# A decoder block in fp32: the MLP's normalized activations at 64 and at 0 modulo 128 bytes

## The chip, the core and the metric

One core of a Trainium2 chip runs the whole kernel. The metric is the device time of one execution in microseconds (us). TensorE (PE in the rows; its weight loads are listed apart as PEld) multiplies, VectorE (DVE) and ScalarE (ACT) do the elementwise work, GpSimd (POOL) helps, and SyncE (SP) issues the transfers.

## What is computed

A decoder block on 256 tokens of width 1024. Cut to the part at hand:

```python
h  = h + rmsnorm(m @ w_out, norm_mix_post)      # after two gated token mixers
u2 = rmsnorm(h, norm_mlp_pre)
a  = square(relu(u2 @ w_up))                    # w_up is 1024 x 4096
h  = h + rmsnorm(a @ w_down, norm_mlp_post)     # w_down is 4096 x 1024
```

## The kernel before, in words

Every fp32 matrix is split into a high and a low part (`..h`, `..l`) of the type fp32r, and each product is made of three matmuls: high by high, high by low and low by high (`mm3`, L223 to L229; `mm3_wide`, L231 to L240, does the same for a row that is 1024 wide). A matmul holds one operand, 128 columns of it, in the array: the stationary operand, which a weight load (LDWEIGHTS) of its own brings in. It then streams the other one, the moving operand, past it. Each matmul here has its weight load; the load for the next matmul runs while the present one streams.

Weights arrive by DMA (`.._r`), ScalarE makes the high part of a block (L89) and VectorE the low part (L93). The queues' orders are written out by hand.

The MLP works on eight chunks `j` of 512 hidden features. For chunks 1 to 7, `up_half` multiplies the weights `up{j}_h/l`, which are stationary, by the activations `u2h/u2l`, which are moving and 256 wide (all tokens): 2 halves x 2 feature tiles x 8 blocks of the contraction x 3 matmuls = 96 matmuls a chunk. The results are squared and split into `ah/al`, with which the down projection (`d_ps`) goes on: there `ah/al` are stationary and the weights `dn` move, 512 wide; the last step of each token tile in the chunks 0 to 5 has four matmuls that are only 256 wide (`mm3_narrow_end`, L250). Chunk 0 (`up_tokens`) is done the other way round: `u2h/u2l` stationary, the weights moving, 512 wide, 48 matmuls.

SBUF is allotted by pools, one tile after another. In the compiled program the address of a tile, in bytes within each partition, is fixed. Modulo 128 these are:

- all split weights (`up`, `dn`, `o`, `p`, `g`, ...): 96
- `uh/ul`, the first norm's activations, moving beside the weights of `q`, `k`, `p` and `g`: 32
- `u2h` and `u2l` (addresses 156,832 and 165,024): 32 and 32
- `ah/al`: 96, behind a tile `gap` of 64 bytes which holds nothing

`placed` makes a tile that is 128 elements too long and returns a view that begins `at` elements of 4 bytes behind its start; `uh/ul` come from it, `u2h/u2l` don't. Every step from one block of the contraction to the next, and every column slice that the matmuls take, is a multiple of 128 bytes, so that these residues hold for all operands of a tile.

Of the kernel before, what the change touches and what calls it, by code (L numbers as in the profile page):

```python
# [9 lines left out]
F32R = mybir.dt.float32r  # L10
# [6 lines left out]
P = 128  # L17
D = 1024
S = 256
NT = S // P  # L20
KD = D // P
# [12 lines left out]
def hybrid_block(ctx: ExitStack, tc: tile.TileContext, x, norm_mix_pre, w_in, b_gate, pool_w, pool_scale,  # L34
# [222 lines left out]
    def wide(blocks, k):  # L257
        b = blocks[k // 2]
        return b.hi[:, k % 2, :], b.lo[:, k % 2, :]
# [2 lines left out]
        b = blocks[k // 4]  # L262
        return b.hi[:, k % 4, c], b.lo[:, k % 4, c]

    def placed(pool, blocks, tag, name, at):


        t = pool.tile([P, blocks * S + 128], F32R, tag=tag, name=name)
        return t[:, at:at + blocks * S].rearrange("p (k s) -> p k s", k=blocks)

    def two(ps):
# [66 lines left out]

    v_sb = mixer.tile([P, NT, AW], F32, name="v_sb")
    u = tuple(placed(act, KD, f"uT_{i}", f"u{i}", 112) for i in "hl")  # L340
    rr = [const.tile([P, 1], F32, name=f"rr{t}") for t in range(NT)]

# [121 lines left out]
    stacked = mixer.tile([P, 2 * H * S + 32], F32R, tag="sg", name="stacked")  # L464
    k2, q2 = (stacked[:, a:a + H * S].rearrange("p (h s) -> p h s", h=H) for a in (0, H * S + 16))
    ql = [placed(mixer, 4, t, f"ql{i}", 112) for i, t in enumerate(("q_yh", "pt2"))]
    own = [slice(i * DH, (i + 1) * DH) for i in range(2)]

# [150 lines left out]
    def pool_project(g2):  # L619
        if not yp:  # L620
            yp.extend(placed(mixer, NG, t, t[2:], a) for t, a in (("q_yh", 32), ("k_yl", 48)))
        ps = bank(f"y_ps{g2}")
        for j in range(2):
            g = 2 * g2 + j
            mm3(ps[:, j * S:(j + 1) * S], (pws[0][:, g, :], pws[1][:, g, :]), (ys[0][:, g, :], ys[1][:, g, :]),
                True, True)
        for j in range(2):
            g = 2 * g2 + j
            v, sc = ps[:, j * S:(j + 1) * S], others[P_SCALE + g]
            nc.scalar.activation(yp[0][:, g, :], v, AF.Copy, scale=sc)  # L630
            nc.vector.scalar_tensor_tensor(yp[1][:, g, :], v, sc, yp[0][:, g, :].bitcast(F32),
                                           op0=ALU.mult, op1=ALU.subtract)
# [79 lines left out]
    for c in range(2):  # L712
        for f2 in range(2):
            f = 4 * c + 2 * f2
# [17 lines left out]
    mix.close()  # L732
    work = ctx.enter_context(tc.tile_pool(name="work", bufs=2))
    h_sb = work.tile([P, NT, D], F32, name="h_sb", bufs=1)
    u2 = tuple(work.tile([P, KD, S], F32R, name=f"u2{i}", bufs=1) for i in "hl")

    work.tile([P, 16], F32, name="gap", bufs=1)

# [52 lines left out]
    def squared_relu(ps, name):  # L791
        r = work.tile([P, 512], F32, tag="relu", name="relu" + name)
        nc.scalar.activation(r, ps, AF.Relu)  # L793
        a = work.tile([P, 512], F32, tag="a", name="a" + name)
        nc.vector.tensor_tensor(a, ps, r, ALU.mult)  # L795
        return a
# [48 lines left out]
    at = squared_relu(p0, "0_0")  # L845
# [5 lines left out]
    at = squared_relu(p1, "0_1")  # L851
# [78 lines left out]
    for n, c in halves():  # L930
        for k in range(4):
            h, l = wide(bd[-1], k)
# [31 lines left out]
```

## Time and profile before

| what | value |
|---|---|
| three runs, median (lowest to highest) | 340.08 us (339.73 to 341.2) |
| the profiled execution, its own time | 340.61 us |
| its span, from the first to the last instruction | 338.8 us |
| mean granted TensorE clock, share of full speed | 0.994 |
| TensorE busy / weight loads busy | 98% / 90% of the span |
| VectorE / ScalarE / GpSimd busy | 65% / 54% / 23% |

The profile describes one execution. The ends of matmuls are modelled and neighbours overlap, so the pace of TensorE is read from the distance between two starts, and not from the busy time of an instruction.

### The profile page before, as it was taken

How to read it: one execution, taken by the hardware profiler on the slowest of the kernel's cores; microseconds unless marked ns; L12 is line 12 of the kernel's file. 1: busy time of each engine (PE TensorE's matmuls, PEld its weight loads, DVE VectorE, ACT ScalarE, POOL GpSimd, SP SyncE). 2: the span in 40 equal slices, each digit the busy share in tenths (PEclk: the TensorE clock that was granted, in tenths of full speed). 3: DMA queues.
4: the chain of work that ended last, by engine and by line, in shares of the span. 5: the costliest groups of instructions: out<-in, count | busy, mean ns of one | idle time of the engine just before them, and what ended most of it. 6: DMA issues, size and time to landing. Idle time of an engine off the chain costs nothing.

```text
span 338.8 us, 5695 instructions
## 1 busy us (share of the span) xinstructions
PE 331.1 (98%) x2325; PEld 306.5 (90%) x2325; DVE 219.4 (65%) x288; ACT 182.3 (54%) x256; POOL 79.0 (23%) x68
## 2 busy tenths in 40 slices
PE   9999999999999999999999999999999999999992
PEld 7799999999999999888898998989989989899881
DVE  3799678996386799366686746637366374663535
ACT  3985677765746755076668526354264451544331
POOL 3699689145305000046700000000000000000000
PEclk9999999999999999999999999999999999999997
DMA  6996971654455946708355763917619267080003
GB/s 215 373 321 217 225 230 32 226 175 146 179 183 194 366 133 227 265 1 250 124 156 217 267 230 121 331 45 257 240 61 323 114 225 273 10 342 24 0 0 124
DMA packets 27362, 63.04 MB, mean 186 GB/s; under 512 B 1316, under 2 KB 2760, under 8 KB 27336
## 3 DMA queue, kind: packets, MB, share of 16 engines
q1 hardware_dynamic: 26760, 62.15, 53.4%
q0 software_dynamic: 576, 0.52, 1.2%
q8 instruction: 18, 0.29, 0.3%
q14 instruction: 8, 0.07, 0.1%
HBM read 61.10 MB, written 1.05 MB: 183 GB/s over the span
## 4 chain that ended last, share of the span: by engine, by line
PE 95%; DMA 2%; SPq 1%; DVE 1%; issue 0%; DVEq 0%; ACT 0%; ACTq 0%
PE up_ps L227 9%; PE up_ps L229 9%; PE up_ps L228 9%; PE d_ps L237 7%; PE d_ps L236 7%; PE d_ps L240 7%; PE g_ps L227 4%; PE g_ps L228 4%; PE g_ps L229 4%; PE wo_ps L240 2%; PE wo_ps L236 2%; PE wo_ps L237 2%; DMA x_sb<-in_x_dram 2%; PE k_ps L229 1%; PE q_ps L227 1%; PE p_ps L229 1%
## 5 line engine op out<-in xcount | busy, mean ns | idle before, releaser
L227 PE MATMUL up_ps<-u2h,up_h 128*128 128x256 f32 x224 | 62.1, 277 | 0.0
L228 PE MATMUL up_ps<-u2l,up_h 128*128 128x256 f32 x224 | 61.9, 276 | 0.0
L229 PE MATMUL up_ps<-u2h,up_l 128*128 128x256 f32 x224 | 61.9, 276 | 0.0
L93 DVE TENSOR_TENSOR dn_l<-dn_r,dn_h 128x2048 fp32r<-128x2048 f32 x16 | 36.5, 2292 | 16.6 <-ACT dn_h L89 16.5
L228 PEld LDWEIGHTS up_ps<-u2l,up_h 128*128 128x128 f32 x224 | 42.1, 188 | 0.0
L227 PEld LDWEIGHTS up_ps<-u2h,up_h 128*128 128x128 f32 x224 | 42.1, 188 | 0.0
L236 PE MATMUL d_ps<-dn_h,ah 128*128 128x512 f32 x108 | 42.1, 389 | 0.0
L237 PE MATMUL d_ps<-dn_l,ah 128*128 128x512 f32 x108 | 42.1, 389 | 0.0
L229 PEld LDWEIGHTS up_ps<-u2h,up_l 128*128 128x128 f32 x224 | 42.1, 188 | 0.0
L89 ACT ACTIVATE dn_h<-dn_r 128x2048 fp32r<-128x2048 f32 x16 | 30.4, 1915 | 21.5 <-issue 12.8
L880 POOL TENSOR_TENSOR o_out<-o_out,g_mlp_post 128x256 f32<-128x256 f32 x1 | 0.7, 737 | 159.1 <-ACT o_out L879 159.1
L227 PE MATMUL g_ps<-uh,g_h 128*128 128x256 f32 x128 | 35.7, 279 | 0.0
L93 DVE TENSOR_TENSOR up_l<-up_r,up_h 128x2048 fp32r<-128x2048 f32 (+1 forms) x14 | 30.2, 2193 | 8.1 <-ACT up_h L89 8.1
L228 PE MATMUL g_ps<-ul,g_h 128*128 128x256 f32 x128 | 35.4, 277 | 0.0
L229 PE MATMUL g_ps<-uh,g_l 128*128 128x256 f32 x128 | 35.4, 277 | 0.0
L240 PE MATMUL d_ps<-dn_h,al 128*128 128x512 f32 x108 | 33.2, 389 | 0.0
L89 ACT ACTIVATE up_h<-up_r 128x2048 fp32r<-128x2048 f32 x16 | 29.9, 1903 | 1.6 <-PE wo_ps L240 1.6
L793 ACT ACTIVATE relu<-up_ps 128x512 f32<-128x512 f32 x16 | 9.5, 597 | 39.2 <-PE up_ps L229 39.2
L795 DVE TENSOR_TENSOR a<-up_ps,relu 128x512 f32<-128x512 f32 x16 | 11.0, 690 | 28.6 <-ACT relu L793 28.5
L93 POOL TENSOR_TENSOR up_l<-up_r,up_h 128x640 fp32r<-128x640 f32 (+1 forms) x4 | 15.6, 3912 | 44.1 <-ACT up_h L89 44.1
L240 PEld LDWEIGHTS d_ps<-dn_h,al 128*128 128x128 f32 x108 | 20.3, 188 | 4.2
L228 PEld LDWEIGHTS g_ps<-ul,g_h 128*128 128x128 f32 x128 | 24.1, 188 | 0.0
(240 smaller groups left out, 859.9 us busy)
## 6 DMA issues: line engine op xcount, KB each, us to landing
up_r<-in_w_up_dram SPq DMA_DIRECT2D x16, 1024.0 KB, 5.7
dn_r<-in_w_down_dram SPq DMA_DIRECT2D x16, 1024.0 KB, 4.9
g_r<-in_w_in_dram SPq DMA_DIRECT2D x8, 1024.0 KB, 5.6
o_r<-in_w_out_dram SPq DMA_DIRECT2D x4, 1024.0 KB, 4.7
v_r<-in_w_in_dram SPq DMA_DIRECT2D x8, 256.0 KB, 5.9
q_r<-in_w_in_dram SPq DMA_DIRECT2D x4, 512.0 KB, 6.3
k_r<-in_w_in_dram SPq DMA_DIRECT2D x2, 1024.0 KB, 5.8
p_r<-in_w_in_dram SPq DMA_DIRECT2D x2, 1024.0 KB
```

Of the source, the lines that this page charges most:

```text
L89: nc.scalar.activation(self.hi[:, s, :], self.raw[:, s, :], AF.Copy)
L93: eng.tensor_tensor(self.lo[:, s, c], self.raw[:, s, c], self.hi[:, s, c].bitcast(F32), ALU.subtract)
L227: nc.tensor.matmul(ps, wh, rh, start=start, stop=False, skip_group_check=True)
L228: nc.tensor.matmul(ps, *second, start=False, stop=False, skip_group_check=True)
L229: nc.tensor.matmul(ps, *third, start=False, stop=stop, skip_group_check=True)
L236: nc.tensor.matmul(ps, xh, wh[:, c], start=start, stop=False, skip_group_check=True)
L237: nc.tensor.matmul(ps, xh, wl[:, c], start=False, stop=False, skip_group_check=True)
L240: nc.tensor.matmul(ps, xl, wh[:, c], start=False, stop=stop, skip_group_check=True)
L793: nc.scalar.activation(r, ps, AF.Relu)
L795: nc.vector.tensor_tensor(a, ps, r, ALU.mult)
L880: nc.gpsimd.tensor_tensor(o[:, 768:D], o[:, 768:D], g_mlp_post[:, 768:D], ALU.mult)
```

## The change

`u2h` and `u2l` become views of longer tiles, from `placed`, which gets a parameter for the number of buffers:

```diff
-    def placed(pool, blocks, tag, name, at):
+    def placed(pool, blocks, tag, name, at, bufs=None):
-        t = pool.tile([P, blocks * S + 128], F32R, tag=tag, name=name)
+        t = pool.tile([P, blocks * S + 128], F32R, tag=tag, name=name, **({"bufs": bufs} if bufs else {}))
         return t[:, at:at + blocks * S].rearrange("p (k s) -> p k s", k=blocks)
...
-    u2 = tuple(work.tile([P, KD, S], F32R, name=f"u2{i}", bufs=1) for i in "hl")
+    u2 = tuple(placed(work, KD, f"u2{i}", f"u2{i}", at, 1) for i, at in (("h", 8), ("l", 24)))
```

The number, kind and order of the instructions stay as they were on every engine. In the compiled program `u2h` begins at byte 156,864 (64 modulo 128) and `u2l` at byte 165,632 (0 modulo 128). The tiles that follow in the pool (`gap`, `ah/al`, `relu`, `a`, `o_out`) move up by 1,024 bytes, which leaves their residues modulo 128 as they were. Nothing else moves.

## Rows read from the trace of the kernel before

**Rows 1.** The page: busy time of each engine, and the chain that ended last.

```profile
PE 331.1 (98%) x2325; PEld 306.5 (90%) x2325; DVE 219.4 (65%) x288; ACT 182.3 (54%) x256; POOL 79.0 (23%) x68
...
PE 95%; DMA 2%; SPq 1%; DVE 1%; issue 0%; DVEq 0%; ACT 0%; ACTq 0%
```

**Rows 2.** What TensorE waited for: us in total, times, longest.

```profile
PE busy L61 <- PEq L950: 0.8, 1, 0.8
PE x_ps L317 <- DMA x_sb<-in_x_dram: 0.3, 1, 0.3
```

**Rows 3.** TensorE's groups by shape: stationary * columns, moving | busy us, mean ns.

```profile
L227 PE MATMUL up_ps<-u2h,up_h 128*128 128x256 f32 x224 | 62.1, 277 | 0.0
L228 PE MATMUL up_ps<-u2l,up_h 128*128 128x256 f32 x224 | 61.9, 276 | 0.0
L229 PE MATMUL up_ps<-u2h,up_l 128*128 128x256 f32 x224 | 61.9, 276 | 0.0
...
L228 PE MATMUL p_ps<-ul,p_h 128*128 128x256 f32 x32 | 9.0, 281 | 0.0
...
L227 PE MATMUL bp_ps<-yh,bp_h 128*128 128x256 f32 x32 | 8.8, 276 | 0.0
...
L250 PE MATMUL d_ps<-dn_h,al 128*128 128x256 f32 x24 | 3.8, 282 | 0.0
```

**Rows 4.** TensorE in order of time, into and through chunk 2: start us, us.

```profile
189.79 0.64 PE L250 MATMUL d_ps<-dn_h,al 128*128 128x256 f32 x4
190.26 0.29 PE L227 MATMUL up_ps<-u2h,up_h 128*128 128x256 f32 x1
190.38 0.28 PE L228 MATMUL up_ps<-u2l,up_h 128*128 128x256 f32 x1
190.50 0.28 PE L229 MATMUL up_ps<-u2h,up_l 128*128 128x256 f32 x1
190.62 0.28 PE L227 MATMUL up_ps<-u2h,up_h 128*128 128x256 f32 x1
...
201.16 0.39 PE L236 MATMUL d_ps<-dn_h,ah 128*128 128x512 f32 x1
```

**Rows 5.** The stretch of rows 4: length, busy time by engine, granted clock, DMA share.

```profile
190.62:201.16 10.54, 10.54 (x95) 10.54 (x94) 5.00 (x4) 3.15 (x3) 0.00 (x0) 1.00 0.94 340
```

**Rows 6.** TensorE in order of time: half of the p projection, then transposes.

```profile
44.06 0.28 PE L227 MATMUL p_ps<-uh,p_h 128*128 128x256 f32 x1
...
49.72 0.27 PE L548 MATMUL t_ps<-ident,prob 128*128 128x128 f32 x1
...
50.26 0.27 PE L550 MATMUL t_ps<-ident,prob 128*128 128x128 f32 x1
```

**Rows 7.** TensorE in order of time: the down projection of chunk 1, 512 wide.

```profile
201.86 0.39 PE L237 MATMUL d_ps<-dn_l,ah 128*128 128x512 f32 x1
...
211.60 0.40 PE L250 MATMUL d_ps<-dn_h,al 128*128 128x256 f32 x2
```

**Rows 8.** TensorE in order of time: chunk 0's second token tile, 512 wide.

```profile
162.05 0.39 PE L227 MATMUL up_ps<-up_h,u2h 128*128 128x512 f32 x1
...
167.31 0.39 PE L229 MATMUL up_ps<-up_h,u2l 128*128 128x512 f32 x1
```

**Rows 9.** The writes of u2: xcount, duration ns min/median/max, first and last start.

```profile
L324 ACT ACTIVATE u2h<-h_ps,others_col x16: 352/366/369, 151.3 to 163.9; 128x128 fp32r<-128x128 f32 x16
L325 DVE SCALAR_TENSOR_TENSOR u2l<-h_ps,others_col,u2h x16: 340/351/352, 151.7 to 164.3; 128x128 fp32r<-128x128 f32 x16
```

**Rows 10.** The longest waits of all engines in the MLP, 190 to 311 us.

```profile
ACT relu L793 <- PE up_ps L229: 39.2, 12, 3.5
DVE a L795 <- ACT relu L793: 25.1, 10, 3.4
```

## The prediction

> **What bounds the kernel now.** I read the page first: TensorE is busy for 98% of the span, and the chain that ended last is TensorE for 95% of it [rows 1]. Then TensorE's own waits: 0.8 us for the program's start and 0.3 us for the first piece of x, and none after that [rows 2]. In the MLP the other engines wait for TensorE and not the reverse: the longest waits are ScalarE's for finished `up_ps` and VectorE's for ScalarE behind it [rows 10]. So a nanosecond more or less in a matmul's pace goes straight into the time, and no other engine is near enough to hide it or to become the bound by a per cent.
>
> Next the pace, which is the distance between starts. In chunk 2 the first matmul of the steady stretch starts at 190.62 us and the down projection at 201.16 [rows 4]. Three of the chunk's 96 matmuls lie before that stretch, so 93 fill it: 10.54 / 93 = 113.3 ns each, at full granted clock (1.00) [rows 5]. The 512-wide matmuls of the down projection go at twice that: from 201.86 to 211.60 there are 43, 9.74 / 43 = 226.5 ns [rows 7]. So 113.3 ns looks like the moving stream's own pace, 0.443 ns a column at either width, with the weight load hidden beside it.
>
> How well it is hidden varies. Half of the p projection, the same shape, takes 49.72 - 44.06 = 5.66 us for 48 matmuls, 117.9 ns each [rows 6]. The mean duration tells the two paces apart too: 276 ns in the branch projection `bp` and in the up projection, 281 ns in p [rows 3]; durations stand 163 ns above the spacing in both. Both have the moving operand at 32 and the weights at 96 modulo 128 bytes, so an address pair alone does not fix the pace: at this pair two paces hold, a fast one and a slow one.
>
> And the address pair matters. At the end of chunk 0's down projection come four 256-wide matmuls with both operands at 96: 282 ns on the mean [rows 3], and the start of the next stage still shows the disturbance: 190.26, 190.38, 190.50, 190.62, which is 0.36 / 3 = 120 ns each, before the pace falls to 113.3 [rows 4]. The 512-wide matmuls tell the same from the other side: with both operands at 96 they go at 226.5 ns, but chunk 0 of the up projection, with the stationary operand at 32 and the moving one at 96, needs 5.26 us for 23, 228.7 ns [rows 8]. [...]
>
> **The change, part by part.** No instruction is added, removed or moved. What changes is the start of two operands modulo 128.
>
> *The 672 matmuls with moving u2* (3 groups of 224 [rows 3], of which 448 stream `u2h` and 224 `u2l`). Before, both lie 64 bytes from the weights; after, both lie 32 bytes from them, on either side. No row of the trace has an fp32r pair at 32 bytes, and every fp32r operand before the change lies at 32 modulo 64, so the price must be bounded. From above: the disturbed pace of rows 4, 120 ns, gives 672 x (120 - 113.3) = 4.5 us. From below, a gain: the shortest spacing of matmuls that each have a weight load is that of the transposes, 128 wide, 49.72 to 50.26 us for 5, 108 ns [rows 6]; if the moving stream had its pace only from its place, the load would be the next bound, and 672 x (113.3 - 108) = 3.6 us would be saved. Between them lies p's slow pace: 672 x (117.9 - 113.3) = 3.1 us lost. I take this one. The nearest rows are those of the same shape, with a load behind every matmul; of these the trace shows 113.3 and 117.9 as paces that last. The fast one has to be held by high and low parts alternately, and after the change these stand on different sides of the weights, so one timing must suit two different pairs; before it had to suit one.
>
> *The 48 matmuls of chunk 0*, where u2 is stationary and the weights move. They now pay 228.7 - 226.5 = 2.2 ns each [rows 7, 8]. At best that vanishes, 0.1 us; at worst I let it triple, 0.2 us lost. I take nothing.
>
> *The 32 writes of u2* by ScalarE and VectorE, 366 and 351 ns [rows 9]. Only the start within 128 bytes changes. TensorE waits for none of them [rows 2]; it has the rest of the output projection and chunk 0's first token tile to do meanwhile. Without that cover, 1% of 32 x 0.36 us is 0.1 us. Nothing.
>
> *The 1,024 bytes* by which `ah/al` and the tiles behind move keep their residues, so the down projection stays at 226.5 ns. Nothing.
>
> **Sum.** The profiled execution took 340.61 us (span 338.8 and 1.8 around it): 340.61 + 3.1 = 343.7. It lay 0.5 us above the median of the runs shown, 340.08, so for the median I say 343.2 us.
>
> **Rivals.** *It makes no difference that can be measured.* The fast pace holds at the new pair too. For it: before the change the up stage starts disturbed at 120 ns and finds back to 113.3 within some matmuls [rows 4], so the fast pace attracts; and 113.3 seems the moving stream's own, whatever stands beside it. Against it: p stays at 117.9 through a whole half without finding back [rows 6]. The time would be 340.1 us; it is also the result, nearly, if only `u2l` is hit: 224 x 4.6 = 1.0 us, 341.1. [...]
>
> *It becomes faster.* All fp32r streams here start in the middle of a 64-byte piece, at 32 modulo 64, and after the change u2 starts at the beginning of one. If the pace of 113.3 ns is due to that, the weight load's 108 ns bounds next: 3.6 us less, 336.5 us; half of it, 338.3. [...] It decides from a saving of 2.5 ns a matmul on. [...]
>
> *It becomes slower by more*: every matmul at the disturbed 120 ns, 344.6 us, or beyond it, where no row reaches. It is the same mechanism with a higher price.
>
> **Chances.** Slower, at p's pace or somewhat around it: 0.46; slower by more than 345.5: 0.06. Together 0.52 for slower by over 0.5% (1.7 us, 2.5 ns on each of the 672; that is about what a measurement of this kernel can tell from no change). No difference within 0.5%: 0.32. Faster: 0.16. The likeliest case alone spans 342 to 344.6 us. For 8 in 10 the range takes in the case of no change and the weaker half of the gain: 338.3 to 345.5 us; it leaves out most of the full gain (about 0.1) and the tail above (0.06).
>
> **What would show it.** In the trace after, the three groups of 224 should have mean durations near 281 ns and chunk 2's 96 matmuls should span about 0.4 us more (11.3 us in place of 10.9); the steps of TensorE between the up stages, 226.5 ns wide, should not move, nor should p or g. If the three groups stay at 276, the rival of no change is right; if the one with `u2l` differs from those with `u2h`, the sides of the weights are not alike and the argument of one timing for two pairs falls. Durations below 274 would show the gain. I am wrong altogether if the time moves while these three groups don't: then it is the writes, or a phase that some other stage enters by chance, as p and g do.

## The result, and the profile after

The changed kernel takes 343.39 us (median of 4 runs, 343.3 to 343.88) against 340.22 us before: a ratio of 1.009, 95% interval 1.0063 to 1.0117. It is slower by 3.2 us; 343.2 us was forecast.

TensorE's share and its waits are as before: 98% busy, and 1.3 us of waits in all; the last row, 0.2 us, is new and lies in the first projection, `v`. ScalarE and VectorE still wait for the up projection, a little longer each time (41.8 / 12 = 3.5 us and 31.0 / 12 = 2.6, against 39.2 / 12 = 3.3 and 25.1 / 10 = 2.5 in [rows 10]). First the page's line, then TensorE's waits, then the two longest waits of the MLP:

```profile
PE 333.6 (98%) x2325; PEld 308.9 (90%) x2325; DVE 219.4 (64%) x288; ACT 182.2 (53%) x256; POOL 79.0 (23%) x68
```

```profile
PE busy L61 <- PEq L949: 0.8, 1, 0.8
PE x_ps L316 <- DMA x_sb<-in_x_dram: 0.3, 1, 0.3
PE v_ps L229 <- DVE v_l L93: 0.2, 1, 0.2
```

```profile
ACT relu L792 <- PE up_ps L229: 41.8, 12, 3.7
DVE a L794 <- ACT relu L792: 31.0, 12, 3.6
```

The pace of the up projection has changed, and hardly anything else in the MLP. TensorE's groups by shape, which answer to [rows 3] (busy us, mean ns):

```profile
L229 PE MATMUL up_ps<-u2h,up_l 128*128 128x256 f32 x224 | 63.0, 281 | 0.0
L228 PE MATMUL up_ps<-u2l,up_h 128*128 128x256 f32 x224 | 63.0, 281 | 0.0
L227 PE MATMUL up_ps<-u2h,up_h 128*128 128x256 f32 x224 | 62.7, 280 | 0.0
L236 PE MATMUL d_ps<-dn_h,ah 128*128 128x512 f32 x108 | 42.1, 390 | 0.0
...
L228 PE MATMUL p_ps<-ul,p_h 128*128 128x256 f32 x32 | 8.9, 279 | 0.0
```

The three groups with moving u2 stand at 280 and 281 ns in place of 276 and 277. The busy column barely shows it (overlapping matmuls count once); the starts do. Chunk 2 in order of time, TensorE only, as in [rows 4]:

```profile
190.43 0.28 PE L227 MATMUL up_ps<-u2h,up_h 128*128 128x256 f32 x1
...
201.76 0.39 PE L236 MATMUL d_ps<-dn_h,ah 128*128 128x512 f32 x1
```

From 190.43 to 201.76 us the chunk's 96 matmuls take 11.33 us, 118.0 ns each; before it was 201.16 - 190.26 = 10.90 us, 113.5. At this price seven chunks lose 7 x 0.43 = 3.0 us, which is nearly the whole change. The clock is not the reason: the same stretch has a granted clock of 1.00, as in [rows 5].

```profile
190.43:201.76 11.33, 11.33 (x98) 11.33 (x97) 5.38 (x4) 3.15 (x3) 0.00 (x0) 1.00 0.84 308
```

Chunk 0, where u2 is stationary, lost a little too. Its second token tile, which answers to [rows 8], needs 166.98 - 161.66 = 5.32 us for 23 matmuls, 231.3 ns in place of 228.7:

```profile
161.66 0.40 PE L227 MATMUL up_ps<-up_h,u2h 128*128 128x512 f32 x1
...
166.98 0.40 PE L229 MATMUL up_ps<-up_h,u2l 128*128 128x512 f32 x1
```

### The profile page after: what moved, and what is told of

Same layout as the page of the kernel before. It is cut to its first block, busy times and chain, and to the rows that moved or that the text cites. A ratio compares the mean times of both kernels' runs of the same rounds, so it can differ in the third digit from the quotient of the medians.

```text
span 341.5 us, 5695 instructions
## 1 busy us (share of the span) xinstructions
PE 333.6 (98%) x2325; PEld 308.9 (90%) x2325; DVE 219.4 (64%) x288; ACT 182.2 (53%) x256; POOL 79.0 (23%) x68
## 3 DMA queue, kind: packets, MB, share of 16 engines
HBM read 61.10 MB, written 1.05 MB: 182 GB/s over the span
## 4 chain that ended last, share of the span: by engine, by line
PE 95%; DMA 2%; SPq 1%; DVE 1%; issue 0%; DVEq 0%; ACT 0%; ACTq 0%
PE up_ps L228 9%; PE up_ps L229 9%; PE up_ps L227 9%; PE d_ps L236 7%; PE d_ps L240 7%; PE d_ps L237 7%; PE g_ps L227 4%; PE g_ps L228 4%; PE g_ps L229 4%; PE wo_ps L240 2%; PE wo_ps L236 2%; PE wo_ps L237 2%; DMA x_sb<-in_x_dram 2%; PE k_ps L229 1%; PE q_ps L227 1%; PE p_ps L228 1%
## 5 line engine op out<-in xcount | busy, mean ns | idle before, releaser
L229 PE MATMUL up_ps<-u2h,up_l 128*128 128x256 f32 x224 | 63.0, 281 | 0.0
L228 PE MATMUL up_ps<-u2l,up_h 128*128 128x256 f32 x224 | 63.0, 281 | 0.0
L792 ACT ACTIVATE relu<-up_ps 128x512 f32<-128x512 f32 x16 | 9.5, 594 | 41.8 <-PE up_ps L229 41.8
```

Of the source, the lines that this page charges most:

```text
L228: nc.tensor.matmul(ps, *second, start=False, stop=False, skip_group_check=True)
L229: nc.tensor.matmul(ps, *third, start=False, stop=stop, skip_group_check=True)
```

## The experiments

Each edit is against the kernel that its text names. "Distance" is that from the moving to the stationary operand, modulo 128 bytes and in either direction. Where both were read, a 256-wide matmul's mean duration stands some 163 ns above its spacing: 276 with 113.3 ns before the change, 281 with 118.0 after it, 283 with 120.0 with both at 96 (nine matmuls in 1.08 us). So a pace given below from a row of groups alone is an estimate by these pairs: 276 is 113.3 ns, 281 is 118, 283 to 284 is 120. Ratios are against runs of the kernel before beside them on the same chip.

**Both at 32, with the change's longer tiles.** Against the changed kernel:

```diff
-for i, at in (("h", 8), ("l", 24)))
+for i, at in (("h", 0), ("l", 0)))
```

> Theory P (the pair): the pace is set by where the moving operand lies relative to the weights, modulo 128 bytes, and the fast pace of 113.3 ns a matmul needs the 64 bytes of before. This kernel has the change's longer tiles and its shift of the later tiles by 1,024 bytes, but u2h and u2l both at 32, as before. P: the three up groups have mean durations of 276 to 277 ns, and the time is that of before, 340.2 us. Rival S (the shift): it is the 1,024 bytes, or the tiles' length, that slowed it: 281 ns and 343.4 us.

Measured: 340.44 us, ratio 0.9997 (0.9981 to 1.0012). The groups of this kernel:

```profile
L227 PE MATMUL up_ps<-u2h,up_h 128*128 128x256 f32 x224 | 62.1, 277 | 0.0
...
L228 PE MATMUL p_ps<-ul,p_h 128*128 128x256 f32 x32 | 8.8, 276 | 0.0
```

The longer tiles and the shift of 1,024 bytes cost nothing; the residues cost all. The reader is to see the second row as well: the p projection, whose addresses no kernel so far has touched, is at 276 ns here, was at 281 before the change [rows 3] and at 279 after it. One pair of addresses has two paces, and which of them holds varies from one profile to another. It varies within a profile too. In the kernel before, a stage of the gates, with `uh/ul` beside weights at 96, runs from the first of these rows to the second:

```profile
86.83 0.36 PE L227 MATMUL g_ps<-uh,g_h 128*128 128x256 f32 x1
...
92.57 0.28 PE L227 MATMUL y_ps<-ys_pws 128*128 128x256 f32 x1
```

It needs 5.74 us for 48 matmuls, 119.6 ns each, and behind its first steps stays at 117.8 to its end (87.15 to 92.45 us for 45). The gates ahead of it, with the same addresses modulo 128, go at 113.4 (79.81 to 84.12 us for 38).

**Both at 64.** `at` is 8 for both:

> u2h and u2l both at 64, 32 bytes below the weights at 96. Theory P: 32 bytes are the wrong distance whichever part has them, so about 281 ns in all three groups and 343.4 us. Rival T (one timing for two pairs): a slow pace comes only because the high and low parts lie on different sides of the weights; with both on one side the pace finds back to 113.3 ns, durations of 276 ns, 340.2 us. Rival A (absolute place): operands that start at 0 modulo 64 are slow as such: 281 ns, 343.4 us, as by P.

Measured: 343.35 us, ratio 1.0086 (1.0052 to 1.0119).

```profile
L227 PE MATMUL up_ps<-u2h,up_h 128*128 128x256 f32 x224 | 63.1, 282 | 0.0
L228 PE MATMUL up_ps<-u2l,up_h 128*128 128x256 f32 x224 | 62.9, 281 | 0.0
```

Rival T falls: on one side of the weights the two parts are as slow as on different sides (343.35 against 343.39 us).

**Both at 96.** `at` is 16 for both:

> u2h and u2l both at 96, the residue of the weights; distance 0, and again at 32 modulo 64 as every operand before the change. Theory P: the wrong distance too; the 256-wide steps at the end of the down projection with this pair showed 118 to 120 ns, so 281 to 283 ns and 343.4 to 344.7 us. Rival A: 32 modulo 64 is a fast place, so 276 ns and 340.2 us.

Measured: 344.95 us, ratio 1.0129 (1.0088 to 1.0169).

```profile
L227 PE MATMUL up_ps<-u2h,up_h 128*128 128x256 f32 x224 | 63.5, 284 | 0.0
```

This is the slower end that the prediction had bounded with 120 ns. The place is at 32 modulo 64, as every operand before the change, so rival A (the absolute place) is in trouble.

**Every address 32 bytes higher.** Against the kernel before:

```diff
 const = ctx.enter_context(tc.tile_pool(name="const", bufs=1))
+const.tile([P, 8], F32, name="shift")
```

> The kernel before with a tile of 32 bytes put ahead of all others, so that every address grows by 32 and every distance stays: weights at 0, moving operands of the narrow projections at 64. Theory P: nothing changes, 276 to 277 ns in the three up groups, 340.2 us. Rival A: all operands now lie at 0 modulo 64, so that not only the 672 matmuls of the up projection but also the 864 narrow ones of q, k, p, the gates and the branches go at 118 ns: 340.2 + 3.1 + (864 - 250 that were slow before) x 4.6 ns = 346 us.

Measured: 340.1 us, ratio 0.9991 (0.9966 to 1.0015). The lines of this kernel are one higher:

```profile
L228 PE MATMUL up_ps<-u2h,up_h 128*128 128x256 f32 x224 | 62.1, 277 | 0.0
```

Rival A falls. Here u2 lies at 64, as `u2h` does after the change, and its groups are fast, 277 ns in place of 280 and 281; the weights have moved with it. It is the distance that counts.

**Both at 0.** `at` is 24 for both:

> u2h and u2l both at 0, 32 bytes above the weights at 96. Theory P (the distance modulo 128 sets the pace, 64 bytes is fast): the other side is slow too, about 118 ns, durations of 281 ns, 343.4 us. Rival D (only the lower side is slow, a place below the weights that the stream reaches first): 276 ns and 340.2 us, and then the change's u2l cost nothing by itself.

Measured: 343.09 us, ratio 1.0062 (1.004 to 1.0084).

```profile
L227 PE MATMUL up_ps<-u2h,up_h 128*128 128x256 f32 x224 | 62.9, 281 | 0.0
L229 PE MATMUL up_ps<-u2h,up_l 128*128 128x256 f32 x224 | 62.9, 281 | 0.0
L228 PE MATMUL up_ps<-u2l,up_h 128*128 128x256 f32 x224 | 62.3, 278 | 0.0
```

Rival D falls too: 32 bytes above the weights cost about what 32 below do (343.09 and 343.35 us).

**One half of the change, then the other.** `at` is 8 and 0 (`u2h` at 64, `u2l` left at 32), then 0 and 24 (`u2h` left at 32, `u2l` at 0):

> One part of the change alone: u2h at 64, u2l still at 32. Theory P, each matmul by its own operands: the 448 matmuls that stream u2h go at about 118 ns and the 224 with u2l at 113.3, 448 x 4.7 = 2.1 us, 342.3 us. Rival L (the loop has one pace, since a matmul hands its timing on to the next): all 672 slow, 343.4 us, or all fast, 340.2 us.

> The other part alone: u2h at 32, u2l at 0. Theory P, each matmul by its own operands: 224 x 4.7 = 1.1 us, 341.3 us, with only the group that streams u2l slow. Rival L: all three groups alike, 343.4 or 340.2 us.

Measured: 342.98 us, ratio 1.006 (1.0038 to 1.0082), and 343.05 us, ratio 1.0088 (1.0058 to 1.0118). The groups of the first, in order of time a stretch of it, and the groups of the second:

```profile
L229 PE MATMUL up_ps<-u2h,up_l 128*128 128x256 f32 x224 | 63.3, 283 | 0.0
L227 PE MATMUL up_ps<-u2h,up_h 128*128 128x256 f32 x224 | 63.1, 282 | 0.0
L228 PE MATMUL up_ps<-u2l,up_h 128*128 128x256 f32 x224 | 62.2, 278 | 0.0
```

```profile
196.75 0.28 PE L227 MATMUL up_ps<-u2h,up_h 128*128 128x256 f32 x1
196.87 0.28 PE L228 MATMUL up_ps<-u2l,up_h 128*128 128x256 f32 x1
...
197.81 0.28 PE L227 MATMUL up_ps<-u2h,up_h 128*128 128x256 f32 x1
```

```profile
L227 PE MATMUL up_ps<-u2h,up_h 128*128 128x256 f32 x224 | 63.2, 282 | 0.0
L228 PE MATMUL up_ps<-u2l,up_h 128*128 128x256 f32 x224 | 62.9, 281 | 0.0
L229 PE MATMUL up_ps<-u2h,up_l 128*128 128x256 f32 x224 | 62.8, 280 | 0.0
```

In the second kernel two of three matmuls keep the fast distance, and all three groups are slow, 280 to 282 ns. So the loss doesn't add up over matmuls; the loop has one pace over its three matmuls (theory L). Either half of the change gives about all of it (342.98 and 343.05 us against 343.39). The first kernel alone would not have decided: three groups of three take 197.81 - 196.75 = 1.06 us, 117.8 ns a matmul, but the matmul with `u2l` is nearly fast there (278 ns, by estimate a pace of 115), so that a price of 119 to 120 ns for each matmul with `u2h` would fit as well.

**Distances between.** `at` is 4 for both (48), then 2 for both (40):

> u2h and u2l both at 48, 48 bytes from the weights: how wide is the fast place? If the pace goes with whole pieces of 32 bytes (rival W), 48 is like 32 and the time is 340.2 us with 276 ns. If the distance counts byte by byte (theory P as it stands), it lies between the fast 64 and the slow 32 bytes: 278 to 279 ns, about 341.8 us.

> u2h and u2l both at 40, 56 bytes from the weights, 8 off the fast place. 48 was slower than 64, so byte distance matters below 32. If the fast place is exact (theory X), this is slow as well, 281 to 283 ns and 343 to 344.5 us. If 16-byte pieces count (rival Y), 40 is like 32: 276 ns and 340.2 us.

Measured: 344.48 us, ratio 1.0101 (1.0076 to 1.0127), and 344.8 us, ratio 1.0123 (1.0106 to 1.0141). One group of each, at 48 and at 40:

```profile
L227 PE MATMUL up_ps<-u2h,up_h 128*128 128x256 f32 x224 | 63.5, 283 | 0.0
```

```profile
L227 PE MATMUL up_ps<-u2h,up_h 128*128 128x256 f32 x224 | 63.6, 284 | 0.0
```

The expectation of a slope between fast and slow was wrong, and so were pieces of 16 or 32 bytes: 8 bytes off the right distance cost as much as the dearest distance tried, 0 bytes (344.95 us).

**The same mistake made elsewhere.** Against the kernel before:

```diff
 u = tuple(placed(act, KD, f"uT_{i}", f"u{i}", 112) for i in "hl")
+act.tile([P, 8], F32, name="shift")
```

> The kernel before with 32 bytes put behind u, so that all that follows grows by 32: the weights lie at 0 and u2 at 64 (64 bytes apart, as before), but u, which moves past the weights of q, k, p and the gates, stays at 32 and is now 32 bytes from them. Theory L (a loop of narrow matmuls has one pace, and it is fast only where each pair in it is 64 bytes apart): the 672 narrow matmuls of q, k, p and the gates go at about 118 ns in place of 113.3 to 114, up to 3.1 us, and 96 wide ones of the output projection lose up to 0.5 us: 342.8 to 343.8 us, with the up groups at 276 ns. Rival U (what was found holds for the up stage alone): 340.2 us.

Measured: 344.29 us, ratio 1.0106 (1.0087 to 1.0125).

```profile
L227 PE MATMUL up_ps<-u2h,up_h 128*128 128x256 f32 x224 | 62.1, 277 | 0.0
...
L227 PE MATMUL g_ps<-uh,g_h 128*128 128x256 f32 x128 | 36.1, 282 | 0.0
...
L227 PE MATMUL ba_ps<-oTh,ba_h 128*128 128x256 f32 x32 | 9.0, 281 | 0.0
```

The gates go at the slow pace, the up projection at the fast one: rival U falls. It is slower than expected by some 0.5 us, and the last row gives a reason. The branch projections `bp` and `ba`, 192 matmuls, keep their 64 bytes, yet they stand at 281 ns in place of 276: 192 x 4.5 = 0.9 us. They come right behind the gates, at 280 to 282 ns here, and seem to have inherited their pace; whether the stage ahead can decide, the next experiment tells.

**The way into the up stage.** Against the kernel before, the narrow end of six down projections made wide (it stands at the last step of the second token tile only, 6 x 4 = 24 matmuls):

```diff
-if j + 2 < NCH and (t, k) == (NT - 1, 3):
+if False:
```

> The kernel before with the four 256-wide matmuls at the end of six down projections made 512 wide, as the others: the up stage is then entered from an undisturbed stream. If the pace of the up stage is fixed by its addresses (theory L), it stays at 113.3 ns, and the disturbance at its start is gone: 24 x 4.8 + 6 x 0.03 us = 0.3 us less, 339.9 us. If the way in decides which pace holds (rival E, as the p projection's change from 117.8 to 113.6 ns between profiles of the same addresses suggests), the up stages may lock at 118 ns: 343.2 us.

Measured: 342.27 us, ratio 1.0054 (1.0036 to 1.0071). Groups, then chunk 2 in order of time:

```profile
L227 PE MATMUL up_ps<-u2h,up_h 128*128 128x256 f32 x224 | 63.1, 281 | 0.0
```

```profile
189.79 0.61 PE L240 MATMUL d_ps<-dn_h,al 128*128 128x512 f32 x2
190.24 0.28 PE L227 MATMUL up_ps<-u2h,up_h 128*128 128x256 f32 x1
...
201.55 0.39 PE L236 MATMUL d_ps<-dn_h,ah 128*128 128x512 f32 x1
```

11.31 us for the 96 matmuls, 117.8 ns each, with u2 at its fast distance. Rival E is right, and theory L in its first form is wrong: the addresses allow the fast pace, but the way in bears on whether it is found. Behind the narrow steps of [rows 4] the stage finds it, without them chunk 2 stays slow to its end; the groups' 281 ns, a mean over all seven chunks, speaks for the same in the other five so entered. Chunk 1 is entered from transposes in both kernels, and its second half keeps 113.3 ns here (174.59 to 179.01 us for 39 matmuls). What in the narrow steps does it isn't shown. A disturbed start alone is not enough: the gates from 86.83 us, shown above, start disturbed too (0.20 us from the first start to the second) and stay at 117.8 ns.

**The wide matmuls.** Against the kernel before:

```diff
-work.tile([P, 16], F32, name="gap", bufs=1)
```

> The kernel before without the 64-byte tile ahead of ah and al: in the down projection the stationary operands move from 96 to 32, 64 bytes from the moving weights. If 64 bytes are the fast distance for every width (rival V), the down projection stays at 226.7 ns or better. By the rows of chunk 0 and v, which are 512 wide at 64 bytes (229.7 ns), and of the down projection at 0 bytes (226.7), the wide ones want distance 0 (theory W): about 372 matmuls x 2.9 ns = 1.1 us slower, 341.3 us, mean durations of 392 ns in place of 389.

Measured: 341.02 us, ratio 1.0023 (1.0008 to 1.0038).

```profile
L236 PE MATMUL d_ps<-dn_h,ah 128*128 128x512 f32 x108 | 42.3, 391 | 0.0
L237 PE MATMUL d_ps<-dn_l,ah 128*128 128x512 f32 x108 | 42.1, 390 | 0.0
L240 PE MATMUL d_ps<-dn_h,al 128*128 128x512 f32 x108 | 33.7, 393 | 0.0
```

The same groups in the kernel before, at distance 0:

```profile
L236 PE MATMUL d_ps<-dn_h,ah 128*128 128x512 f32 x108 | 42.1, 389 | 0.0
L237 PE MATMUL d_ps<-dn_l,ah 128*128 128x512 f32 x108 | 42.1, 389 | 0.0
L240 PE MATMUL d_ps<-dn_h,al 128*128 128x512 f32 x108 | 33.2, 389 | 0.0
```

Without the gap they stand at 390 to 393 ns in place of 389; the kernel loses 0.0023 x 340 = 0.8 us in all. Some 0.3 us of that is not theirs: the up projection's three groups, at unchanged addresses, are busy for 62.2 + 62.0 + 62.0 = 186.2 us here and 62.1 + 61.9 + 61.9 = 185.9 before. So the 512-wide matmuls were fastest at distance 0, where 256-wide ones go at 120 ns. Rival V falls. Chunk 0 of the up projection, 512 wide too, has the third distance: the mean duration of its group with `up_l` is 390 ns at 0 bytes (both at 96), 391 at 64 (before), 394 and 395 at 32 (both at 64, both at 0).

None of these kernels beats the one before.

## Why the prediction was right, point by point

- *What bounds.* TensorE took the loss whole; no other engine hid any of it. Chunk by chunk the 0.43 us agrees with the forecast of 0.4.
- *The price of the 672 matmuls.* The forecast took p's slow pace, 117.9 ns; measured were 118.0 on the stretch of chunk 2. Both kinds of distance at 32 bytes show it (281 and 282 ns with both at 64, 278 and 281 with both at 0). The upper bound of 120 ns was the right one for distance 0 (120.0 measured), and by the durations of 283 and 284 ns also for `u2` at 40 and at 48.
- *The reason given for choosing it* was wrong in part. The step "one timing must suit two different pairs" fell: with both parts on one side the pace is the same. What the runs put in its place: of the distances tried, only 64 bytes for every pair of the loop let the up stage reach 113.3 ns, and besides it takes a way in that leads there. One pair off (224 of 672 matmuls) is enough to lose it for all. That the price came out to 0.1 ns is therefore luck in part: p's slow pace belongs to the fast distance, no row told that 32 bytes would cost the same, and other wrong distances cost about 120 ns.
- *"An address pair alone does not fix the pace"* was right, and is now shown rather than read from p: the kernel with the wide end holds 117.8 ns at the fast distance. It also undoes the forecast that p would not move: after the change a part of p found the fast pace (281 to 279 ns; its second half goes at 113.6 ns after the change and at 117.8 before), with its addresses as before.
- *Chunk 0* was put at nothing, at worst 0.2 us lost; it lost 48 x 2.6 = 0.1 us. Whether it is the load or the stream that makes a matmul there take 228.7 ns in place of 226.5 isn't shown; a load's record there lasts 188 ns. *The writes of u2* cost nothing: their medians are 367 and 350 ns after the change, 366 and 351 before [rows 9]. *The 1,024 bytes*: nothing, shown by the kernel with both at 32.
- *The rivals.* No change fails: the address matters to these fp32r streams, and 8 bytes off the fast distance (`u2h` and `u2l` at 40) cost 1.2%. The rival of a gain from starts at 0 modulo 64 falls with the kernel whose addresses all grew by 32: weights and u2 there start at 0 modulo 64, and the groups stand at 277 and 276 ns as before. (The 108 ns that bounded this gain is not quite the shortest spacing with a load each: the warm-up matmuls in bf16 stand 107 ns apart, 1.05 to 2.98 us for 18.) The rival of a higher price, 120 ns, is what 0, 48 and 56 bytes cost, but not 32.

What stays open: why 64 bytes, and where the places of the two operands come to bear on each other; no record shows it. Nor whether it is the weight load that is hidden less at a slow pace: the median of its record is 188 ns before and after the change, 192 with both at 96. Nor what makes a way in lead to the fast pace. Two ways in were there in each kernel with `u2` at a wrong distance (chunk 1 behind transposes, the others behind narrow steps), and none is seen to have led to 113.3 ns: the halves of chunk 1 go at 117.8 and 119.8 ns after the change, and the lowest mean of an up group in the others is 278 ns (both at 0, and `u2h` alone at 64), against 276. Whether yet another way in would lead there was not tried. That the distance counts modulo 128 bytes, and not modulo a longer stretch, is not shown either: no run moved an operand by just 128 bytes. The kernel with both at 32 moved `u2l` by 512 against the weights, which changed nothing.

## What to carry to other kernels

Where TensorE is the bound and every matmul has a weight load behind it, read the distance between starts, not the busy time (98% of the span here before and after); a pace that differs at one shape and clock can come from where the operands lie (113.3 against 118.0 ns here), or from the stage ahead (113.3 against 117.8). Change the distance of the moving to the stationary operand modulo 128 bytes for all tiles of a loop together, since here one tile off cost nearly as much as both (342.98 and 343.05 us against 343.39), and try it for each width by itself: here 256-wide matmuls were fastest at 64 bytes (276 and 277 ns against 278 to 284), 512-wide ones at none (389 against 390 to 393 in the down projection). An odd shape at the end of the stage before may be what lets a stage find its fast pace (taking out the narrow end cost 0.5% here); measure before removing it.

## What was not expected of the hardware

- The steady paces of 256-wide fp32r matmuls with a load each, where starts were read, are 113.3 to 113.6 ns or 117.8 to 120.0. At 64 bytes those of q, p, the gates, the branches and the up projection are 113.3 to 113.6 or 117.8. Eight bytes off the fast distance already give 283 and 284 ns, by estimate 120 between starts.
- The stage ahead bears on the pace. At an unchanged distance of 64 bytes the branch projections went at 281 ns in place of 276 behind slow gates, and the up projection at 281 in place of 276 and 277 with six of its stages behind an undisturbed 512-wide stream.
- The matmuls 512 wide order 0 and 64 bytes the other way round: mean durations in the down projection of 389 ns at 0 bytes, and 390 to 393 at 64.
- A pace of its own per stage may explain part of the spread between runs, which is not shown: the p projection alone had mean durations of 281, 279 and 276 ns in the profiles of three kernels in which its addresses were the same.
